# Stick-breaking attention: sigmoid(-z) scanned in SBUF instead of PSUM, and part of the weight splitting moved from VectorE to GpSimd

## The chip, the cores and the metric

The kernel runs on one core of a Trainium2 chip. Its metric is the device time of one execution, in microseconds (us), as the median of several executions; lower is better. Five engines matter: TensorE (PE in the profile; its weight loads are PEld), VectorE (DVE), ScalarE (ACT), GpSimd (POOL) and SyncE (SP), which issues the DMAs. Each takes its own instructions in a fixed order. Matmul results lie in PSUM (eight banks of 512 fp32 columns), everything else that the engines work on in SBUF.

## The reference

One layer of a streaming encoder, for 2048 prompt rows and for 128 sample rows (8 streams of 16) with a cache of 512 past positions. The input is normed, modulated and projected; two attention branches run side by side (A: differential attention; B: stick-breaking attention with 8 heads of 64); both are gated, merged, projected and normed. The change touches branch B alone:

```python
def stick_breaking_attention(q, k, v, qpos, kpos):
    z = jnp.einsum('bqhd,bkhd->bhqk', q, k) * (HEAD_DIM_B ** -0.5)
    mask = kpos[None, :] < qpos[:, None]
    log_1m = jnp.where(mask, jax.nn.log_sigmoid(-z), 0.0)
    log_a = jax.nn.log_sigmoid(z) + lax.cumsum(log_1m, axis=3, reverse=True) - log_1m
    a = jnp.where(mask, jnp.exp(log_a), 0.0)
    return jnp.einsum('bhqk,bkhd->bqhd', a, v)
```

The weight of key j is thus sigmoid(z_j) times the product of sigmoid(-z_i) over all later visible keys i. The kernel forms that product as a scan (a running product) from the last key to the first.

## The kernel before

**Order of the work.** A first phase (up to about 150 us) forms the modulated input and writes it to DRAM. The main loop (to about 1810 us) has eight units: four pairs of a branch-A unit (one head) and a branch-B unit (two heads). Each unit walks over the sample tile and then the 16 prompt tiles t = 0 to 15 of 128 rows. Tile t attends to t + 1 blocks of 128 keys, so late tiles are long. A last phase (to the end) does the sample attention, the branch and output projections and the final norm. One step of the main loop interleaves three streams: the projections of a tile some steps ahead (`project`, whose lead is reckoned by `LEAD` and by `duration`), the scores of the present tile (`scores`), and the product of weights and values of the tile two steps back (`pv`, `PV_LAG`). So towards the end of a B unit the projections are those of the next A unit. The framework then draws up each engine's order with a timeline of its own, from the order in which the program emits.

**One tile of a B unit.** For each of two heads `c`, chunks of 512 keys run from the last to the first. Per chunk, two matmuls (lines 639 and 640; on the diagonal also the mask, line 643) put z into a PSUM bank of the kind "s", of which there are three. `evacuate` (line 549) lets ScalarE write sigmoid(z) to the SBUF tile `seg["p"]` (line 562) and sigmoid(-z) back over z in PSUM (line 563). `stick` (line 606) lets VectorE scan that PSUM bank in reverse into the SBUF tile `seg["n"]` (line 616); the second operand of the scan is `zero_t`, one SBUF column read over and over. The bank is free once the scan has read it.

**Weights.** Every 1024 keys make a segment (`SEG` = 8 blocks), so tiles from t = 8 on have two segments for each head. Once a segment and the one after it are scanned, `stick_weights` (line 619) lets GpSimd multiply `p` by the scanned `n`, one column further (line 622). `turn` (line 565) then splits the product into two fp16 halves, written into the space of `n`: ScalarE copies the high half (line 572), VectorE subtracts to get the low half (line 573). SP issues a transposing DMA of both into `wt` (line 580), which the matmuls of `pv_block` (lines 700 and 701) read. The tiles `p` and `n` have six buffers each (`SC_BUFS`); a tile from t = 8 on takes four of each.

**Other users of these engines.** A projection for an A unit rotates queries and keys with three GpSimd instructions (lines 469, 471, 474) and splits them on VectorE (lines 463 and 295, from `rot` in SBUF); a projection for a B unit splits them straight from PSUM (`ps_mm`). GpSimd also multiplies each B output by its gate (line 683). SP's queue holds, among the transposes, the loads of the modulated input for the next projection (`hs`, line 405). In branch A, ScalarE and VectorE make the weights and GpSimd has no part in them.

## Time and profile before

| What | Value |
|---|---|
| Time, median of 3 runs | 2347.12 us (2343.01 to 2352.8) |
| Profiled execution, its own time | 2352.01 us |
| Its span, first to last instruction | 2350.2 us |
| Mean granted TensorE clock | 0.965 |
| PE busy in the span | 2124.9 us (90%) |
| DVE, ACT, POOL busy | 1725.1, 1644.4, 705.0 us |

The page gives each engine's busy time, then groups of instructions by source line: how many, how long in all, the mean of one, and how long the engine stood idle before them and what ended that. A busy PE may still be waiting inside, since matmuls are pipelined. Busy times of DVE and POOL include time in which an instruction has begun but is held up. A window view gives the busy times within a stretch of the span; a source view gives the shortest, median and longest duration of the instructions of one line.

### The profile page before, as it was taken

What the parts mean: (1) busy time and instruction counts of PE and PEld (TensorE: products, weight loads), DVE (VectorE), ACT (ScalarE), POOL (GpSimd) and SP (SyncE); (2) the same over time, 40 slices, a digit from 0 to 9 for tenths busy, and PEclk for the clock granted to TensorE, in tenths of its full rate; (3) what the DMA queues carried; (4) which work ended last, traced back from release to release, by engine and by line L of the source; (5) the groups of instructions that cost most, each with busy time, mean ns of one, the idle gap of its engine ahead of it and who ended that gap; (6) DMA issues with size and microseconds to landing.
All of it is one profiled execution on the core that took longest, in us unless ns stands there. A gap on an engine that the chain in (4) does not pass through costs nothing. (4 is left out here: it accounts for less than half of the span.)

```text
span 2350.2 us, 42700 instructions
## 1 busy us (share of the span) xinstructions
PE 2124.9 (90%) x15272; PEld 1144.5 (49%) x15272; DVE 1725.1 (73%) x3652; ACT 1644.4 (70%) x3260; POOL 705.0 (30%) x610
## 2 busy tenths in 40 slices
PE   5898899998999999899999979998996879988998
PEld 3554454444555445445545545554553344544443
DVE  4848866779875667978667797877688877777663
ACT  4557878787886778878677777866777656665541
POOL 1533012446300334731033474103335111221111
PEclk8999899999999999999999999999996989999999
DMA  9766759887895988867577787766687999999531
GB/s 334 252 203 177 165 127 263 180 188 163 207 227 131 213 199 189 175 175 191 139 188 175 186 171 185 192 146 149 142 175 162 288 238 250 237 249 243 157 103 48
DMA packets 834357, 445.34 MB, mean 189 GB/s; under 512 B 537210, under 2 KB 777130, under 8 KB 833632
## 3 DMA queue, kind: packets, MB, share of 16 engines
q1 hardware_dynamic: 833196, 442.24, 76.5%
q8 instruction: 119, 1.95, 0.3%
q14 instruction: 94, 0.77, 0.1%
q10 hardware_dynamic: 948, 0.39, 0.1%
HBM read 245.60 MB, written 69.24 MB: 134 GB/s over the span
## 5 line engine op out<-in xcount | busy, mean ns | idle before, releaser
L622 POOL TENSOR_TENSOR sc_p<-sc_p,sc_n 128x127 f32<-128x127 f32 (+7 forms) x192 | 314.2, 1640 | 834.8 <-DVE sc_n L616 812.5
L428 PE MATMUL ps_mm<-wb,hs 128*128 128x512 f16 x1632 | 412.1, 380 | 5.1 <-DMA hs<-hT_d 3.0
L428 PEld LDWEIGHTS <-hs 128*128 128x128 f16 x3120 | 275.8, 99 | 264.5 <-issue 14.8
L428 PE MATMUL ps_mm<-wa,hs 128*128 128x512 f16 x1488 | 377.7, 384 | 9.0 <-DVE qbuf L463 3.8
L616 DVE TENSOR_TENSOR_SCAN sc_n<-ps_s,sc_n,zero_t 128x512 f32<-128x512 f32 x192 | 245.5, 1279 | 80.8 <-ACT ps_s L119 77.5
L639 PE MATMUL ps_s<-k,qst 128*128 128x512 f16 (+3 forms) x640 | 227.5, 356 | 37.2 <-DVE sc_n L616 25.8
L573 DVE TENSOR_TENSOR sc_n<-sc_p,sc_n 128x128 f16<-128x128 f32 (+7 forms) x192 | 211.5, 1106 | 51.8 <-ACT sc_n L572 51.3
L504 PEld LDWEIGHTS <-hs 128*128 128x128 f16 x1632 | 155.6, 98 | 181.4 <-DVE qst L532 5.5
L119 ACT ACTIVATE sc_p<-ps_s,usc 128x512 f32<-128x512 f32 (+3 forms) x320 | 204.3, 638 | 35.3 <-PE ps_s L640 27.9
L640 PE MATMUL ps_s<-k,qst 128*128 128x512 f16 (+3 forms) x640 | 227.1, 356 | 0.0
L572 ACT CAST sc_n<-sc_p 128x128 f16<-128x128 f32 (+7 forms) x192 | 154.9, 811 | 78.9 <-POOL sc_p L622 76.0
L700 PE MATMUL ps_o<-v,wt 128*128 128x128 f16 x1088 | 172.2, 226 | 35.1 <-DMA wt<-sc_n 35.1
L119 ACT ACTIVATE ps_s<-ps_s,usc 128x512 f32<-128x512 f32 (+3 forms) x328 | 199.4, 608 | 0.0
L504 PE MATMUL ps_t<-wb,hs 128*128 128x512 f16 x816 | 192.9, 380 | 2.5 <-DVE qst L532 2.2
L504 PE MATMUL ps_t<-wa,hs 128*128 128x512 f16 x816 | 192.3, 381 | 3.1 <-DVE qst L532 2.2
L1341 PE MATMUL ps_o<-wo,wb 128*128 128x512 f16 x816 | 189.2, 386 | 4.0 <-ACT wb L1163 4.0
L701 PE MATMUL ps_o<-v,wt 128*128 128x64 f16 x1088 | 158.3, 198 | 0.0
L700 PEld LDWEIGHTS <-wt 128*128 128x128 f16 x1088 | 105.6, 101 | 100.1 <-DMA wt<-sc_n 46.4
L558 DVE TENSOR_SCALAR_CACHE_REDUCE sc_n<-ps_s,usc 128x512 f32<-128x512 f32 (+3 forms) x160 | 106.5, 666 | 42.2 <-PE ps_s L640 22.9
L616 DVE TENSOR_TENSOR_SCAN sc_n<-ps_s,zero_t 128x128 f32<-128x128 f32 (+3 forms) x128 | 104.2, 815 | 41.0 <-ACT ps_s L119 38.0
L558 DVE TENSOR_SCALAR_CACHE_REDUCE sc_p<-ps_s,usc 128x512 f32<-128x512 f32 (+3 forms) x160 | 106.4, 665 | 35.6 <-PE ps_s L640 26.1
L701 PEld LDWEIGHTS <-wt 128*128 128x128 f16 x1088 | 103.4, 101 | 54.5 <-issue 1.9
(358 smaller groups left out, 4531.3 us busy)
## 6 DMA issues: line engine op xcount, KB each, us to landing
hs<-hT_d SPq DMA_DIRECT2D x130, 512.0 KB, 4.4
g_d<-gt SPq DMA_DIRECT2D x68, 256.0 KB, 4.4
wb<-g_d SPq DMA_DIRECT2D x26, 512.0 KB, 5.7
out_dram<-pr SPq DMA_DIRECT2D x204, 64.0 KB, 2.4
o_d<-o SPq DMA_DIRECT2D x136, 64.0 KB, 2.0
hs<-o_d SPq DMA_DIRECT2D x17, 512.0 KB, 5.1
out_dram<-x SPq DMA_DIRECT2D x17, 512.0 KB, 2.8
wide<-in_w_ada_dram SPq DMA_DIRECT2D x8, 1024.0 KB, 7.8
```

What stands on the lines that cost most here:

```text
L119: i = S.activation(**kw)
L428: T.matmul(box["p"], box["h"][:, hi, k, :], U["w"][k][:, wi, :], start=(n == 0), stop=(n == 3 * KT - 1))
L504: T.matmul(box["g"][:, 0:gw], box["h"][:, hi, k, :], U["wg"][k // per][:, k % per, wi, :], start=(j == 0), stop=(j == 3 * KT - 1))
L558: V.tensor_scalar(out=dst[:, lo : lo + n], in0=p[:, 0:n], scalar1=sc_pos, scalar2=None, op0=ALU.mult, op1=ALU.max, accum_out=job["mx"][:, ...
L573: V.tensor_tensor(out=lo, in0=src, in1=hi, op=ALU.subtract)
L616: V.tensor_tensor_scan(out=dst[:, lo : lo + n][:, ::-1], data0=src[:, 0:n][:, ::-1], data1=zero_t[:, 0:1].to_broadcast([P, n]), initial=fi ...
L622: G.tensor_tensor(out=p[:, 0:m], in0=p[:, 0:m], in1=n[:, 1 : m + 1], op=ALU.mult)
L639: T.matmul(p[:, 0:n], qst[:, c, :], kk[:, c, 0:n], start=True, stop=False)
L640: T.matmul(p[:, 0:n], qst[:, 2 + c, :], kk[:, c, 0:n], start=False, stop=not diag)
L700: T.matmul(po[:, c * P : (c + 1) * P], wt[:, wj, :], vt[:, c, :, :], start=first, stop=False)
L701: T.matmul(po[:, c * P : c * P + 64], wt[:, nb + wj, :], vt[:, c, 0, :], start=False, stop=last)
L1341: T.matmul(po, st["y"][:, yi * 8 + k, :], wo[j * 4 + k // 2][:, wi, k % 2, :], start=(n == 0), stop=(n == 3 * KT - 1))
```

## The change

`evacuate` writes sigmoid(-z) to `seg["n"]` in SBUF, ahead of sigmoid(z), and no longer back into PSUM. `stick` loses its operand `src` and scans `seg["n"]` in place; its second operand is `zero_t` as before. In `turn`, for the second head (`c == 1`) of prompt tiles from t = 8 on, GpSimd subtracts the low half in place of VectorE. The same `evacuate` and `stick` serve the sample tile of the last phase, where the subtraction stays on VectorE.

```diff
         else:
 
+            act(out=seg["n"][:, lo : lo + n], in_=p[:, 0:n], func=AF.Sigmoid, scale=sc_neg)
             act(out=seg["p"][:, lo : lo + n], in_=p[:, 0:n], func=AF.Sigmoid, scale=sc_pos)
-            act(out=p[:, 0:n], in_=p[:, 0:n], func=AF.Sigmoid, scale=sc_neg)
...
             S.copy(out=hi, in_=src)
-            V.tensor_tensor(out=lo, in0=src, in1=hi, op=ALU.subtract)
+
+            (G if job["c"] == 1 and 8 <= job["t"] < NT else V).tensor_tensor(out=lo, in0=src, in1=hi, op=ALU.subtract)
...
-    def stick(seg, later, lo, n, src):
+    def stick(seg, later, lo, n):
...
-        V.tensor_tensor_scan(out=dst[:, lo : lo + n][:, ::-1], data0=src[:, 0:n][:, ::-1], data1=zero_t[:, 0:1].to_broadcast([P, n]),
+        x = dst[:, lo : lo + n][:, ::-1]
+        V.tensor_tensor_scan(out=x, data0=x, data1=zero_t[:, 0:1].to_broadcast([P, n]),
                              initial=first, op0=ALU.mult, op1=ALU.add)
...
-            stick(seg, later, ch * 512 - seg["lo"] * P, n, p)
+            stick(seg, later, ch * 512 - seg["lo"] * P, n)
...
-                    stick(seg, None, 512, P, pn[:, c * P : (c + 1) * P])
-                    stick(seg, None, 0, 512, pc)
+                    stick(seg, None, 512, P)
+                    stick(seg, None, 0, 512)
```

## The prediction

> **What bounds the kernel now.** I began with the page: engine totals and the costliest groups.

> ```profile
> PE 2124.9 (90%) x15272; PEld 1144.5 (49%) x15272; DVE 1725.1 (73%) x3652; ACT 1644.4 (70%) x3260; POOL 705.0 (30%) x610
> ...
> L639 PE MATMUL ps_s<-k,qst 128*128 128x512 f16 (+3 forms) x640 | 227.5, 356 | 37.2 <-DVE sc_n L616 25.8 <-DVE sc_p L558 7.8 <-DVE sc_n L558 3.1
> ...
> L119 ACT ACTIVATE sc_p<-ps_s,usc 128x512 f32<-128x512 f32 (+3 forms) x320 | 204.3, 638 | 35.3 <-PE ps_s L640 27.9 <-PE ps_s L643 6.9
> ...
> L119 ACT ACTIVATE ps_s<-ps_s,usc 128x512 f32<-128x512 f32 (+3 forms) x328 | 199.4, 608 | 0.0
> ```

> Over the whole span PE is busiest, and its waits for a PSUM bank that a scan still holds come to 25.8 us. An average hides stages, so next I asked for windows: tiles 8 to 12 of the first B unit, then tiles 13 to 15 of each of the four.

> ```profile
> 415.00:503.90 88.90, 84.20 (x569) 43.45 (x568) 62.41 (x102) 67.38 (x136) 33.33 (x26) 1.00 0.85 177
> 503.90:565.00 61.10, 51.20 (x421) 28.54 (x419) 59.13 (x66) 49.77 (x93) 41.95 (x30) 0.97 0.88 175
> 926.80:988.00 61.20, 50.54 (x424) 28.04 (x422) 58.76 (x65) 49.43 (x92) 44.67 (x32) 0.97 0.89 179
> 1341.40:1405.00 63.60, 52.71 (x451) 29.70 (x448) 60.56 (x65) 49.96 (x92) 44.63 (x32) 1.00 0.87 188
> 1754.30:1808.00 53.70, 32.14 (x283) 19.43 (x281) 51.16 (x61) 43.74 (x72) 33.69 (x20) 0.71 0.78 156
> ```

> Columns: length, then PE, PEld, DVE, ACT, POOL busy, granted clock. In the first row PE bounds (84 of 89). In the four late rows DVE does: 59.13 of 61.10, while PE idles 10 to 22 us each. The waits of the first late window, and PE's in the last, say the same:

> ```profile
> PE ps_s L639 <- DVE sc_n L616: 5.2, 7, 1.1
> PE ps_t L517 <- DVE k L295: 4.5, 3, 2.0
> ...
> PE ps_o L700 <- DMA wt<-sc_n: 14.9, 10, 3.2
> ```

> So the change is decided in these four stretches of three tiles, and there by DVE with POOL.

> **The rows that matter most: who blocks whom.** The source views (shortest, median, longest ns) of four kinds of DVE instruction:

> ```profile
> L616 DVE TENSOR_TENSOR_SCAN sc_n<-ps_s,sc_n,zero_t x192: 1265/1282/1285, 353.5 to 1801.2; 128x512 f32<-128x512 f32 x192
> L295 DVE SCALAR_TENSOR_TENSOR v<-ps_mm,usc,v x136: 318/344/352, 72.5 to 1747.7; 128x128 f16<-128x128 f32 x136
> L295 DVE SCALAR_TENSOR_TENSOR k<-rot,sq,k x68: 331/346/2089, 76.9 to 1503.0; 128x128 f16<-128x128 f32 x68
> L573 DVE TENSOR_TENSOR sc_n<-sc_p,sc_n x192: 266/1093/3052, 331.5 to 1808.3; 128x1024 f16<-128x1024 f32 x80, 128x128 f16<-128x128 f32 x16, 128x256 f16<-128x256 f32 x16, 128x384 f16<-128x384 f32 x16
> ```

> The first two read one tensor from PSUM and one from SBUF; they never vary. The last two read both from SBUF, and go from 346 to 2089 ns. The timelines of POOL and DVE show why (start, duration):

> ```profile
> 517.37 1.53 POOL L622 TENSOR_TENSOR sc_p<-sc_p,sc_n 128x767 f32<-128x767 f32 x1
> ...
> 525.63 1.77 POOL L622 TENSOR_TENSOR sc_p<-sc_p,sc_n 128x895 f32<-128x895 f32 x1 [0.30 <-DVE sc_n L616]
> ...
> 538.94 0.45 POOL L683 TENSOR_TENSOR o<-o,gt 128x128 f32<-128x128 f32 x1
> 539.92 2.76 POOL L622 TENSOR_TENSOR sc_p<-sc_p,sc_n 128x1024 f32<-128x1024 f32 x1 [0.54 <-DVE sc_n L616]
> 542.97 0.73 POOL L469 TENSOR_TENSOR rot<-pr,rope 128x256 f32<-128x256 f32 x1 [0.28 <-ACT pr L442]
> ...
> 546.44 2.00 POOL L622 TENSOR_TENSOR sc_p<-sc_p,sc_n 128x1023 f32<-128x1023 f32 x1 [1.73 <-DVE sc_n L616]
> ```
> ```profile
> 539.77 1.06 DVE L573 TENSOR_TENSOR sc_n<-sc_p,sc_n 128x896 f16<-128x896 f32 x1
> ...
> 546.73 2.79 DVE L573 TENSOR_TENSOR sc_n<-sc_p,sc_n 128x1024 f16<-128x1024 f32 x1
> ...
> 565.23 1.21 DVE L573 TENSOR_TENSOR sc_n<-sc_p,sc_n 128x1024 f16<-128x1024 f32 x1
> ```

> At 546.44 POOL is first and keeps its 2.00; the subtraction takes 2.79 in place of 1.21 and ends 1.08 after POOL. At 539.77 DVE is first; now POOL takes 2.76 and ends 1.85 after it. They take turns, whole instructions at a time, and hide some 0.14 us of each: a path into SBUF that both need. Today the scan does not need it. After the change it reads `sc_n` and `zero_t`, both in SBUF.

> [...]

> **Part 1: the scan in SBUF.** Its own length I keep: 1282 ns from PSUM, and the 128-wide splits take 344 from PSUM and 346 from SBUF. What it costs is its turn on the shared path. The windows of the scans' line and of the low halves' line (L573), DVE busy and count:

> ```profile
> 415.00:503.90 88.90, 35.12 (x33) 1.00 0.85 177
> 503.90:565.00 61.10, 28.50 (x24) 0.97 0.88 175
> ...
> 415.00:503.90 88.90, 17.75 (x20) 1.00 0.85 177
> 503.90:565.00 61.10, 19.43 (x11) 0.97 0.88 175
> 926.80:988.00 61.20, 21.36 (x12) 0.97 0.89 179
> 1341.40:1405.00 63.60, 24.41 (x12) 1.00 0.87 188
> 1754.30:1808.00 53.70, 15.49 (x12) 0.71 0.78 156
> ```

> The path's demand in one late window, each instruction at its undisturbed length less 0.14:
> - 24 scans: 28.5 - 3.4 = 25.1 (new on this path)
> - 12 POOL products: 8 x 2.00 + 2 x 1.77 + 2 x 1.53 = 22.6, less 1.7 = 20.9
> - 6 low halves left to DVE: 4 x 1.21 + 1.06 + 0.9 = 6.8, less 0.8 = 6.0
> - 15 rotations of the next A unit at 0.73: 8.9; its 10 splits at 0.34: 2.0; 4 output products at 0.45: 1.2

> **Part 2: six low halves on POOL.** DVE loses as many as it keeps. For POOL the nearest row subtracts fp16 from fp32 in the first phase:

> ```profile
> L1099 POOL TENSOR_TENSOR hp<-tmp,hp x40: 421/1156/1204, 42.2 to 141.2; 128x512 f16<-128x512 f32 x32, 128x128 f16<-128x128 f32 x8
> ```

> 421 ns for 128 and 1156 for 512 make about 2.1 us for 1024, beside 2.00 for a product. At the product's price six cost 11.3 - 0.8 = 10.5; at the dearer one 0.6 more a window.

> **Sum.** 25.1 + 20.9 + 6.0 + 8.9 + 2.0 + 1.2 + 10.5 = 74.6 us of demand against windows of 61.1, 61.2 and 63.6: +13.5, +13.4, +11.0. The last unit has no A projections behind it, 74.6 - 10.9 = 63.7 against 53.7: +10.0. In all **+48**. Tiles 8 to 12 of the first unit: scans 35.1 - 33 x 0.14 = 30.5, POOL at most 33.3, its new subtractions at most half as much again less 1.4 = 15.3, DVE's remaining low halves 17.75 / 2 = 8.9; 88.0 of 88.9, and less in truth, as those busy times include waiting. So full but not over: 0, at most +5 a unit.

> **What eases or adds to it.** A bank is now free after ScalarE's second sigmoid, so PE and ACT may run ahead of DVE until the six buffers are full: one and a half tiles, half a tile more than the one in work, about 10 us (61.1 / 3 / 2) a unit or 40 in all. But PE also waits for DVE's splits (4.5 above), which queue behind scans; I take half, -20. On POOL a low half must first wait for ACT's copy:

> ```profile
> 534.24 1.05 ACT L572 CAST sc_n<-sc_p 128x1024 f16<-128x1024 f32 x1 [0.68 <-POOL sc_p L622]
> ```

> Behind it in POOL's queue stand the next product and the rotations, for which ACT and DVE, then PE's transposes wait. Six times 1.05 is 6.3 a window, 25 in all, nothing if DVE fills the gap: I take half, +12. The transposing DMA starts later, and SP holds loads of `hs` behind it:

> ```profile
> SPq L580 <- DVE sc_n L573: 89.7, 55, 7.6
> ```
> ```profile
> L428 PE MATMUL ps_mm<-wb,hs 128*128 128x512 f16 x1632 | 412.1, 380 | 5.1 <-DMA hs<-hT_d 3.0
> ```

> PE lost 3.0 us to `hs` in that group of 1632, so a microsecond more is covered by the lead of those loads: 0; if it were not, this row would grow first. ScalarE's first sigmoid now ends in SBUF, 638 in place of 608 ns: 24 x 0.03 = 0.7 us a window on an engine with 49.8 of 61.1 busy, hidden by DVE's lag. That the scan may start one sigmoid sooner is worth nothing while DVE is late. The framework draws up every engine's order anew; no row prices that, and the width of the range has to hold it.

> [...]

> The profiled execution took 2352.0, so 2352.0 + 48 - 20 + 12 = 2392.0; it stands 4.9 above the median of the runs shown, 2347.1, so I forecast **2387**. Ends: 48 - 40 = +8 (all of the running ahead counts, no copy is waited for) gives 2355; 48 + 25 + 20 = +93 (no running ahead, every copy waited for, 5 lost in each unit's tiles 8 to 12) gives 2440.

> **The rivals.**
> 1. *The scan does not join the turns* (a one-column operand might not count as a stream). Then only part 2 acts where it was short. DVE sheds its six low halves with their waiting, 19.43 x 6 / 11 = 10.6, 10.7, 12.2 and 7.7 us, and POOL takes 11.3: 53.3, 56.0, 55.9 and 45.0 busy. POOL now bounds the first three windows: -7.8, -5.2, -7.7; in the last PE waits for transposes anyway (14.9), half of 7.7: -4. That is -25, **2322**. It decides if a scan beside a product stays at 1.28 us. For it: the scan never varied so far, and its one-column operand was in SBUF already. Against it: every quoted form with two SBUF tensors stretches.
> 2. *The turns are taken but absorbed*: PE runs ahead through freed banks, +8 at the most favourable, **2355** or less, within 0.5%. For it: the first window row, where PE bounds and DVE has 26 us to spare, and 5.2 us of bank waits that vanish. Against it: a queue cannot serve 74.6 us in 61, and the splits for PE's next projections stand in that queue.
> 3. *POOL becomes the bound as well* through copies it waits for: **2440** and more. For it: POOL's busy time of 42 to 45 with 11.3 to come. Against it: DVE can use the path meanwhile.
> 4. *The bank is not free sooner*, because ScalarE waits for a buffer of `n`, which the transposing DMA gives back later than now. Then the -20 is gone: 2407, inside the forecast's range.

> **How the numbers follow.** A difference under 0.5%, about 12 us, is what a measurement of this kernel can hardly tell from none. Forecast, 4 included (2360 to 2440): 0.62. Beyond 2440 (3): 0.04. Absorbed (2): 0.14. No turns for the scan (1): 0.20. So slower 0.66, same 0.14, faster 0.20. As both signs have weight, the range reaches from 2318, by rival 1, to 2440; it leaves out 0.04 above and some 0.1 below.

> **What would show it.** Right: the scan's source view goes from 1265/1285 to a longest near 3 us, stretched ones beside a POOL product; the products' and the new POOL subtractions' longest lies near 3 as well; windows of tiles 13 to 15 grow by 10 to 14 us each and DVE stays near 97% busy; the row <-DVE sc_n L616 vanishes from PE's waits, and <-DVE k L295 grows. Wrong: scans stay at 1.28 and the late windows shrink below 57 us (rival 1); scans stretch but PE is not idle longer (rival 2). What would make the forecast wrong altogether is a cost elsewhere: the windows of tiles 0 to 7, or the first and last phase, changing by more than a few us.

## The result and the profile after

The changed kernel took **2469.32 us** (median of 4 runs, 2462.56 to 2474.68) beside 2346.73 of the kernel before: a ratio of 1.0518, 95% interval 1.0484 to 1.0553. That is 122.6 us slower, where 40 had been forecast. The profiled executions differ by 116.0 (spans 2466.2 and 2350.2).

From the page of the changed kernel: engine totals, then groups (busy, mean ns | idle before, and what ended it).

```profile
PE 2166.4 (88%) x15272; PEld 1164.8 (47%) x15272; DVE 1854.3 (75%) x3588; ACT 1650.6 (67%) x3260; POOL 881.0 (36%) x674
...
L618 DVE TENSOR_TENSOR_SCAN sc_n<-sc_n,zero_t 128x512 f32<-128x512 f32 (+3 forms) x320 | 489.5, 1534 | 120.7 <-ACT sc_n L119 111.4
...
L641 PE MATMUL ps_s<-k,qst 128*128 128x512 f16 (+3 forms) x640 | 230.6, 361 | 24.5 <-ACT sc_p L119 11.8
L572 ACT CAST sc_n<-sc_p 128x128 f16<-128x128 f32 (+7 forms) x192 | 154.2, 807 | 142.7 <-POOL sc_p L624 142.1
```

The bank wait on the scan (25.8 before) is gone from the scores' row, as forecast. TensorE is busy 41.5 us longer with the same 15272 instructions, and it is idle for 74.5 more; together that is the 116.0. The scan's source view and those of the low halves (shortest, median, longest ns) show the turns:

```profile
L618 DVE TENSOR_TENSOR_SCAN sc_n<-sc_n,zero_t x320: 393/1284/3161, 327.0 to 1911.5; 128x512 f32<-128x512 f32 x88, 128x128 f32<-128x128 f32 x24, 128x256 f32<-128x256 f32 x24, 128x384 f32<-128x384 f32 x24
...
L574 POOL TENSOR_TENSOR sc_n<-sc_p,sc_n x64: 474/2128/3111, 428.3 to 1921.8; 128x1024 f16<-128x1024 f32 x36, 128x128 f16<-128x128 f32 x4, 128x256 f16<-128x256 f32 x4, 128x384 f16<-128x384 f32 x4
```

The longest scan is 3161 ns where none was over 1285. To place the loss I cut the trace at the first scan of a tile. First the kernel before, unit 1 (the first B unit): tiles 0 to 12, then 13 to 15 (from the first of their scans to the last; the columns are those of the prediction's windows, whose late ones had begun and ended a little differently).

```profile
328.36:503.87 175.51, 165.70 (x1104) 85.96 (x1103) 118.00 (x211) 138.49 (x297) 61.50 (x51) 0.99 0.88 204
503.87:562.80 58.93, 49.03 (x396) 27.12 (x394) 56.96 (x64) 49.73 (x92) 39.93 (x29) 0.97 0.87 175
```

And the changed kernel, the same for all four units:

```profile
327.01:511.01 184.00, 169.92 (x1104) 87.48 (x1103) 137.78 (x203) 138.22 (x296) 80.69 (x60) 0.96 0.83 194
511.01:581.96 70.95, 53.99 (x414) 30.34 (x411) 66.44 (x57) 48.43 (x89) 59.53 (x34) 0.90 0.70 145
773.30:964.15 190.85, 171.03 (x1098) 87.21 (x1096) 138.60 (x204) 137.52 (x294) 81.03 (x59) 0.96 0.78 182
964.15:1035.19 71.04, 54.27 (x417) 30.10 (x416) 69.15 (x56) 48.78 (x89) 60.93 (x34) 0.90 0.73 153
1224.24:1408.40 184.16, 166.99 (x1079) 85.41 (x1078) 137.95 (x205) 130.96 (x280) 81.17 (x59) 0.97 0.68 165
1408.40:1479.47 71.07, 55.46 (x436) 30.90 (x434) 68.83 (x56) 48.88 (x89) 60.95 (x34) 0.93 0.78 163
1664.50:1850.33 185.83, 163.32 (x1073) 84.20 (x1072) 144.58 (x212) 117.21 (x249) 84.36 (x59) 0.98 0.60 140
1850.33:1914.28 63.95, 30.32 (x257) 18.83 (x256) 62.26 (x49) 41.10 (x66) 47.36 (x22) 0.70 0.51 104
```

| us longer than before, by unit | 1 | 3 | 5 | 7 | sum |
|---|---|---|---|---|---|
| tiles 0 to 12 | 8.5 | 13.3 | 14.9 | 18.0 | 54.6 |
| tiles 13 to 15 | 12.0 | 11.8 | 8.8 | 15.8 | 48.4 |

The late windows cost 48.4, close to the 48 of the sum (part of that is luck, as the experiments show). Beside them stand 54.6 us in tiles 0 to 12, and DVE is not full there: 138 of 184. Of these, 29.5 fall in tiles 0 to 7, where the prediction had nothing, and 25.1 in tiles 8 to 12, where it had at most 20. The last 13.0 of the 116.0 lie outside these windows. TensorE's longest waits (us, times, longest), first in the kernel before:

```profile
PE ps_o L700 <- DMA wt<-sc_n: 35.1, 24, 5.2
...
PE ps_t L517 <- DVE k L295: 12.1, 11, 2.0
...
PE ps_mm L428 <- DMA hs<-hT_d: 4.5, 3, 2.6
...
PE ps_t L517 <- ACT gt L507: 3.3, 5, 1.1
```

And in the changed kernel:

```profile
PE ps_o L702 <- DMA wt<-sc_n: 50.8, 25, 7.2
PE ps_t L517 <- DVE k L295: 40.4, 14, 5.8
...
PE ps_mm L428 <- DMA hs<-hT_d: 20.9, 9, 4.3
PE ps_t L504 <- DVE qst L532: 16.1, 11, 3.4
...
PE ps_t L517 <- ACT gt L507: 11.9, 9, 3.1
```

The last of these can be followed in the timeline of tile 10, unit 1 (start, duration, wait before it):

```profile
461.88 1.89 POOL L574 TENSOR_TENSOR sc_n<-sc_p,sc_n 128x384 f16<-128x384 f32 x1
...
462.92 1.93 DVE L618 TENSOR_TENSOR_SCAN sc_n<-sc_n,zero_t 128x512 f32<-128x512 f32 x1
...
465.00 2.00 POOL L624 TENSOR_TENSOR sc_p<-sc_p,sc_n 128x1024 f32<-128x1024 f32 x1 [1.22 <-DVE sc_n L618]
...
467.03 1.04 ACT L572 CAST sc_n<-sc_p 128x1024 f16<-128x1024 f32 x1 [4.53 <-POOL sc_p L624]
467.98 0.68 ACT L507 ACTIVATE gt<-ps_t,usc 128x512 f32<-128x512 f32 x1
...
468.71 0.27 PE L517 MATMUL ps_t<-id,k 128*128 128x128 f16 x2 [3.07 <-ACT gt L507]
```

A low half delays a scan, the scan the product, the product ScalarE's copy; behind that copy stands the evacuation of the gate's bank, for which TensorE waits 3.07. The gate's matmuls had ended at 462.1, and the scan's own stretch in this chain is only 0.65 (1.93 for 1.28); the rest of the 3.07 is the place of the evacuation behind the copy. My first theory (A) was therefore: turns in all tiles, passed on through queues. Its rivals: part 2's longer GpSimd queue (B), the earlier release of banks and the engines' new order (D; the order alone is later F).

### The profile page after: what moved, and what is told of

Read it like the earlier page. It is cut to its first block, busy times and chain, and to the rows that moved or that the text cites. A ratio compares the mean times of both kernels' runs of the same rounds, so it can differ in the third digit from the quotient of the medians.

```text
span 2466.2 us, 42889 instructions
## 1 busy us (share of the span) xinstructions
PE 2166.4 (88%) x15272; PEld 1164.8 (47%) x15272; DVE 1854.3 (75%) x3588; ACT 1650.6 (67%) x3260; POOL 881.0 (36%) x674
## 5 line engine op out<-in xcount | busy, mean ns | idle before, releaser
L624 POOL TENSOR_TENSOR sc_p<-sc_p,sc_n 128x127 f32<-128x127 f32 (+7 forms) x192 | 326.1, 1702 | 736.4 <-DVE sc_n L618 578.1
L618 DVE TENSOR_TENSOR_SCAN sc_n<-sc_n,zero_t 128x512 f32<-128x512 f32 (+3 forms) x320 | 489.5, 1534 | 120.7 <-ACT sc_n L119 111.4
L428 PE MATMUL ps_mm<-wb,hs 128*128 128x512 f16 x1632 | 419.2, 387 | 14.7 <-DMA hs<-hT_d 11.7
L428 PEld LDWEIGHTS <-hs 128*128 128x128 f16 x3120 | 278.6, 100 | 284.0 <-issue 25.0
L428 PE MATMUL ps_mm<-wa,hs 128*128 128x512 f16 x1488 | 383.1, 389 | 12.0 <-DMA hs<-hT_d 9.2
L641 PE MATMUL ps_s<-k,qst 128*128 128x512 f16 (+3 forms) x640 | 230.6, 361 | 24.5 <-ACT sc_p L119 11.8
L572 ACT CAST sc_n<-sc_p 128x128 f16<-128x128 f32 (+7 forms) x192 | 154.2, 807 | 142.7 <-POOL sc_p L624 142.1
L119 ACT ACTIVATE sc_n<-ps_s,usc 128x512 f32<-128x512 f32 (+3 forms) x320 | 203.2, 635 | 34.1 <-PE ps_s L642 16.2
L702 PE MATMUL ps_o<-v,wt 128*128 128x128 f16 x1088 | 178.6, 231 | 50.9 <-DMA wt<-sc_n 50.8
L119 ACT ACTIVATE sc_p<-ps_s,usc 128x512 f32<-128x512 f32 (+3 forms) x320 | 204.6, 639 | 0.0
L702 PEld LDWEIGHTS <-wt 128*128 128x128 f16 x1088 | 110.5, 105 | 119.6 <-DMA wt<-sc_n 63.1
L574 DVE TENSOR_TENSOR sc_n<-sc_p,sc_n 128x1024 f16<-128x1024 f32 (+7 forms) x128 | 150.6, 1178 | 21.7 <-ACT sc_n L572 21.7
L574 POOL TENSOR_TENSOR sc_n<-sc_p,sc_n 128x128 f16<-128x128 f32 (+7 forms) x64 | 135.0, 2110 | 31.5 <-ACT sc_n L572 31.5
L558 DVE TENSOR_SCALAR_CACHE_REDUCE sc_n<-ps_s,usc 128x512 f32<-128x512 f32 (+3 forms) x160 | 106.3, 665 | 42.9 <-PE ps_s L642 29.6
L469 POOL TENSOR_TENSOR rot<-pr,rope 128x256 f32<-128x256 f32 x68 | 68.6, 1009 | 192.1 <-ACT pr L442 137.5
L1351 POOL TENSOR_TENSOR x<-m,x 128x512 f32<-128x512 f32 x34 | 49.7, 1464 | 240.0 <-DVE m L1347 156.7
```

Of the source, the lines that this page charges most:

```text
L119: i = S.activation(**kw)
L428: T.matmul(box["p"], box["h"][:, hi, k, :], U["w"][k][:, wi, :], start=(n == 0), stop=(n == 3 * KT - 1))
L572: S.copy(out=hi, in_=src)
L574: (G if job["c"] == 1 and 8 <= job["t"] < NT else V).tensor_tensor(out=lo, in0=src, in1=hi, op=ALU.subtract)
L618: V.tensor_tensor_scan(out=x, data0=x, data1=zero_t[:, 0:1].to_broadcast([P, n]), initial=first, op0=ALU.mult, op1=ALU.add)
L624: G.tensor_tensor(out=p[:, 0:m], in0=p[:, 0:m], in1=n[:, 1 : m + 1], op=ALU.mult)
```

## The experiments

**The parts alone.** Part 1 alone is the changed kernel with

```diff
-            (G if job["c"] == 1 and 8 <= job["t"] < NT else V).tensor_tensor(out=lo, in0=src, in1=hi, op=ALU.subtract)
+            V.tensor_tensor(out=lo, in0=src, in1=hi, op=ALU.subtract)
```

and part 2 alone the kernel before with the reverse edit.

> Part 1 alone: the scan in SBUF, every low half left on VectorE. Theory A (the scan takes turns with GpSimd, and through GpSimd's late products ScalarE's queue and then TensorE are held up): nearly the whole loss stays. The path's demand in a late window falls by the low halves' difference only (six at 1.9 to six at 1.1), so 65 to 110 us over the kernel before, 2410 to 2455; scans' longest near 3 us, high-half copies of ScalarE waiting for the product 110 to 140 us in all. Rival B (the loss in tiles 0 to 12 comes from GpSimd's longer queue, part 2): only the late windows lose, at most 48 us, so 2370 to 2395, and tiles 0 to 12 stand as before.

> Part 2 alone: sigmoid(-z) and the scan as in the kernel before (scan from PSUM), but from tile 8 on GpSimd subtracts the low halves of the second head's weights. Theory A (the scan's turns are the loss): no loss; VectorE sheds six low halves in each late window, and by the first rival of the prediction the time is 2322, or with copies waited for up to 2347. Rival B (GpSimd's longer queue is the loss): 30 us or more slower than before, 2377 and up, with the high-half copies' wait on GpSimd's products grown as in the changed kernel (142).

Part 1 took 2443.52 (ratio 1.0383, 1.0358 to 1.0407): 91 slower, as A had it. Part 2 took 2369.73 (1.0066, 1.0043 to 1.0090): 17 slower, and neither theory had that. Its late windows did shrink, by 18 in all, but all the rest grew by 39. Whether these 39 belong to the part or to the engines' new order, the runs below settle.

**Do the two SBUF operands make the turns?** A pair with two score banks; in the second kernel the freed bank holds the scan's zero.

```diff
-    BANKS = {"mm": 2, "s": 3, "t": 1, "o": 2}
+    BANKS = {"mm": 2, "s": 2, "t": 1, "o": 2}
...
+    zero_p = ps.tile([P, 512], F32, tag="z", name="ps_z", bufs=1)
+    V.memset(zero_p[:, 0:1], 0.0)
...
-... data1=zero_t[:, 0:1].to_broadcast([P, n]),
+... data1=zero_p[:, 0:1].to_broadcast([P, n]),
```

> The changed kernel with two score banks in place of three, to free one bank; a control for the next run. The bank is free after the second sigmoid, so two may do: both theories expect the changed kernel's time or up to 30 us more (2465 to 2500), scans' longest near 3 us.

> As the control, but the scan's second operand, the repeated zero, is a column in PSUM (in the freed bank), so the scan reads one tensor from SBUF and one from PSUM and writes SBUF. Theory A (two SBUF operands make it take turns, the repeated column counting as one): the scan is back at 1.26 to 1.30 us, shortest to longest, though it reads and writes sc_n in SBUF, and the time falls by 60 us or more against the control. Rival C (reading and writing the same SBUF tensor, or any SBUF read of a long tensor beside GpSimd, makes it wait): scans still reach near 3 us, and the time is the control's within 15 us.

The control took 2520.33, the kernel with the zero in PSUM 2426.04. In the two traces TensorE, ScalarE and GpSimd run the same instructions in the same order (VectorE has the one memset more). The scan's source view, control first:

```profile
L618 DVE TENSOR_TENSOR_SCAN sc_n<-sc_n,zero_t x320: 398/1284/3140, 346.6 to 1966.2; 128x512 f32<-128x512 f32 x88, 128x128 f32<-128x128 f32 x24, 128x256 f32<-128x256 f32 x24, 128x384 f32<-128x384 f32 x24
```
```profile
L620 DVE TENSOR_TENSOR_SCAN sc_n<-sc_n,ps_z x320: 395/1268/1282, 346.7 to 1876.4; 128x512 f32<-128x512 f32 x88, 128x128 f32<-128x128 f32 x24, 128x256 f32<-128x256 f32 x24, 128x384 f32<-128x384 f32 x24
```

With one column moved to PSUM no scan is stretched, and 94 us go. So here a column repeated from SBUF counts as a second SBUF operand, and rival C falls. The 94 hold for the order of this pair.

**The same with three banks: a probe that brought its own wait.** To keep three score banks, the zero was put into an unused column of an output bank; in two further kernels the SBUF column stayed in tiles 13 to 15, or in 0 to 12, and a last one took part 1 alone.

```diff
+        zero = o_ring[0][:, 511:512]           (the two: zero_t[:, 0:1] if 13 <= t < NT, or if t < 13)
...
-... data1=zero_t[:, 0:1].to_broadcast([P, n]),
+... data1=zero.to_broadcast([P, n]),
```

> The changed kernel whole, with its three score banks, but the scan's repeated zero is one unused column of an output bank in PSUM. Theory A (the turns of the scan with GpSimd are the loss, in all tiles): scans 1.26 to 1.30 us throughout, and the time falls by 85 us or more against the changed kernel, to 2345 to 2385. Rival D (a good part is lost by what else the change does, the bank that is given back sooner and the new order of the engines): 2400 or more although no scan is stretched.

> As the run before, but in tiles 13 to 15 the scan's zero is the SBUF column again, so scans take turns in these tiles alone. Theory A: the late windows alone give the prediction's 48 us and some half-clock time on top, 45 to 75 over the run before; tiles 0 to 12 as in the run before.

> The reverse: SBUF column in tiles 0 to 12, PSUM column from 13 on. Theory A (in tiles 0 to 12 the path is not full, but late products, splits and transfers stop TensorE there all the same): 40 to 70 over the run with PSUM everywhere. The prediction's step (these tiles lose nothing, as the path has time to spare): at most 10 over it.

> Part 1 alone without the turns: sigmoid(-z) and the scan in SBUF, the scan's zero in PSUM, every low half on VectorE. Theory A: the score bank comes free one scan sooner and nothing is paid for it: 2325 to 2350, at or under the kernel before. Rival D: 2370 or more.

They took 2487.70, 2481.62, 2468.67 and 2513.13, far off A's numbers; D's (2400 or more, and 2370 or more) were met, but the waits in the first of them show another cause. VectorE's, then TensorE's:

```profile
DVE sc_n L630 <- PE ps_o L715: 81.5, 51, 4.3
```
```profile
PE ps_o L714 <- DVE sc_n L630: 39.0, 32, 3.4
```

No scan was stretched (1282 ns at most), but scans now waited 51 times for the matmuls that write other columns of that bank, and the matmuls 32 times for them. These four therefore decide nothing about the turns or about D.

**One order for both.** The framework draws up each engine's order anew for every kernel. So the next four hold it fixed: an edge without a wait from each instruction to the next of the order wanted, on all five engines (the two sigmoids of a chunk stand in each other's place, as the change has them; the 64 low halves that change engine find their own place).

```diff
+    for each engine, for each instruction i of the order kept, last before it:
+        tc.add_manual_dep(i, last.name, NOSYNC, reason="order kept")
```

> The changed kernel, made to keep the order of the kernel before on every engine (edges without a wait fix each engine's order; the 64 low halves on GpSimd find their own place). Theory A (the turns of the scan with GpSimd are the bulk, at 94 of 122 by the pair with the zero in PSUM; the rest is the engines' new order): 85 to 110 over the kernel before, 2430 to 2460, some 15 to 35 under the changed kernel. Rival F (the order is half or more of it): 2410 or less. Rival G (the order is nothing): 2465 to 2475.

> Part 1 alone (scan in SBUF, every low half on VectorE) in the order of the kernel before, the same on all engines to the last instruction. So what differs is the scan's operands and the earlier release of the bank. Theory A: 70 to 95 over the kernel before (part 1 alone in its own order was 90 over). Rival F: 50 or less.

> Part 2 alone (from tile 8 on GpSimd subtracts the second head's low halves; the scan from PSUM) in the order of the kernel before. In its own order it was 17 slower, with late windows 18 shorter and more TensorE time at half clock. Theory A (those 17 come of the new order, and the part itself saves VectorE time in the late windows): 2335 to 2352. Rival H (the part itself costs, through low halves that wait in GpSimd's queue): 2360 or more.

> The kernel before with the order of the changed kernel on every engine, and nothing else of the change. Theory A: 15 to 40 slower than the kernel before, with waits for hs and for the gate's bank in tiles 0 to 12 as in the changed kernel. Rival G (the order is nothing): within 8 of it.

| kernel | own order, us more | order of the kernel before, us more (ratio, 95%) |
|---|---|---|
| part 1 | 90.6 | 49.5 (1.0212, 1.0181 to 1.0243) |
| part 2 | 16.8 | -4.9 (0.9987, 0.9972 to 1.0002) |
| both | 122.6 | 67.9 (1.0286, 1.0262 to 1.0311) |

The kernel before, in the order of the changed kernel, took 2382.64: 30.0 more (1.0131, 1.0105 to 1.0157).

The new order alone costs 30.0 where no scan takes turns, and 54.7 on top of the change (48.9 if the two medians, 2469.32 and 2420.47, are taken directly; the kernel before took 2346.73 beside the one and 2352.62 beside the other). So the order is 40 to 45 in a hundred of the loss: for both parts together neither A's range (2430 to 2460) nor F's (2410 or less) was met. Part 2's 17 were order: without it the part makes no difference that can be measured, and that run is also the nearest there is to a control of the edges themselves. In the order of before the windows of unit 1 are

```profile
328.30:504.98 176.68, 165.59 (x1100) 85.83 (x1098) 136.01 (x202) 138.34 (x296) 83.61 (x60) 0.99 0.85 202
504.98:576.76 71.78, 54.00 (x413) 30.57 (x414) 66.55 (x59) 50.03 (x93) 59.62 (x34) 0.88 0.70 145
```

The late windows are +12.9, +13.4, +11.3 and +17.4 longer, 54.9 in all; tiles 0 to 12 only +1.2, -0.6, +4.0 and +3.0. Cut the same way, the profiled executions give, in us more than the kernel before over all four units:

| kernel | tiles 0 to 7 | 8 to 12 | 13 to 15 | the rest | sum |
|---|---|---|---|---|---|
| changed kernel | 29.5 | 25.1 | 48.4 | 13.0 | 116.0 |
| both parts, order of before | 4.8 | 2.8 | 54.9 | 0.4 | 62.9 |
| kernel before, order of the changed kernel | 18.6 | 4.4 | -11.1 | 16.1 | 28.0 |

The last two rows do not add up to the first: 25 us come only when both are there. Two of TensorE's waits do part. The one for hs is 2.1 in the second row's kernel and 16.0 in the third's, so it goes with the order; the one for VectorE's splits is 49.4 and 10.3, so it goes with the change.

**Late tiles or all tiles, in that order.** The scan in SBUF under a condition on the tile, from PSUM otherwise; part 2 whole.

```diff
+            inner = 13 <= job["t"] < NT        (the other kernel: job["t"] < 13)
...
+                             data0=x if inner else src[:, 0:n][:, ::-1],
```

> The whole of part 2, but the scan in SBUF in tiles 13 to 15 alone (elsewhere from PSUM, as before), in the order of the kernel before on every engine. With the scan from PSUM everywhere this order took 2348, with it in SBUF everywhere 2420. Theory A (the late windows are over-full, the others are not): 45 to 65 over the kernel before, 2398 to 2418. Rival I (once the order is the same, the cost is spread over all tiles): 2385 or less.

> The reverse in the same order: the scan in SBUF in tiles 0 to 12 alone. Theory A, and the prediction's own step (at most 5 a unit in tiles 8 to 12, nothing in 0 to 7): 0 to 20 over the kernel before, 2350 to 2372. Rival I: 2385 or more.

They took 2406.46 (1.0243, 1.0223 to 1.0263) and 2359.26 (1.0043, 1.0028 to 1.0058): +56.8 and +9.6, both as A had it, and their sum is the 67.9 of both to within 2. Rival I falls. Unit 1 of each:

```profile
329.64:505.65 176.01, 165.27 (x1100) 85.70 (x1098) 114.33 (x202) 138.03 (x296) 73.63 (x60) 0.99 0.86 203
505.65:577.42 71.77, 52.81 (x404) 29.72 (x405) 66.55 (x59) 49.98 (x93) 59.61 (x34) 0.88 0.71 145
```
```profile
328.17:506.34 178.17, 165.89 (x1104) 86.10 (x1103) 135.59 (x202) 138.72 (x297) 83.56 (x60) 0.99 0.85 201
506.34:562.20 55.86, 48.36 (x409) 27.21 (x407) 49.01 (x59) 49.09 (x92) 47.28 (x34) 1.00 0.87 184
```

In tiles 0 to 12 VectorE is 21.3 us longer busy with turns (135.59 against 114.33) and the stretch only 2.2 longer: in this order something else covers the turns, and in the changed kernel's it does not.

**What in the new order costs?** In the kernel before with the new order, the wait for hs is 16.0 where it was 4.5:

```profile
PE ps_mm L431 <- DMA hs<-hT_d: 16.0, 8, 4.4
```

So each load of hs was set two places earlier in SyncE's queue, the changed kernel's order being otherwise kept.

```diff
 SyncE's kept order, for each load of hs (L405):
-    ..., transfer, transfer, load of hs, ...
+    ..., load of hs, transfer, transfer, ...
```

> The changed kernel in its own order on every engine, except that each load of hs stands two places earlier in SyncE's queue, which takes it past one transposing transfer or store that waits. Theory J (much of what the new order costs in tiles 0 to 12 are loads of hs that stand behind waiting transfers; TensorE waits 20.9 for them there, 16.4 more than in the kernel before, and half as much again is lost to the half clock): 10 to 30 faster than the changed kernel, 2440 to 2460, and that wait at most 10. Rival K (those waits only take the place of others): within 8 of 2469, the wait for the gate's bank or for the splits grown by as much.

2546.61 (1.0850, 1.0824 to 1.0876): some 75 slower than the changed kernel, which neither J nor K had. TensorE's wait for hs did go, from 20.9 to 2.0, but SyncE now stands longer at the load, until a gate's matmuls give an hs buffer back, and the transposing transfers behind it are late. SyncE's row of the changed kernel, then of this one, and below them this one's rows of TensorE's waits:

```profile
SPq L405 <- PE ps_t L504: 78.5, 25, 8.1
```
```profile
SPq L408 <- PE ps_t L507: 163.4, 41, 12.5
```
```profile
PE ps_o L705 <- DMA wt<-sc_n: 90.5, 37, 7.2
...
PE ps_mm L431 <- DMA hs<-hT_d: 2.0, 1, 2.0
```

The wait for wt stood at 50.8 in the changed kernel. So two places in one queue are worth more than the whole late-window effect, and a wait that goes with the order need not be what the order costs. Which engine's order carries the 30 and the 55 stays **open**: no run changed the order of one engine other than SyncE.

## Why the prediction was wrong

The scan's turns, the mechanism of the forecast, were right; the step that failed is the engines' new order, which the sum put at nothing. Step by step:

- **The scan joins the turns** (an inference from the two subtracting forms, as both of its operands would lie in SBUF; no row of the kernel before showed it): right, shown by the pair with the zero in PSUM (3140 ns at the longest with the column in SBUF, 1282 without). Rival 1 is out.
- **"In all +48"**: right in the order of before for three units: the late windows grew by 12.9, 13.4 and 11.3 against 13.5, 13.4 and 11.0. The last unit's 10.0 was mis-sized: it measured 17.4, and 14.6 with part 1 alone in that order (62.75 against 48.19), so the excess comes mostly with the scan; why stays open. In the changed kernel the 48.4 is in part luck: there the new order by itself shortens these windows by 11.1.
- **"Full but not over: 0, at most +5 a unit"** for tiles 8 to 12, and the windows of tiles 0 to 7 unchanged: right in the order of before (7.6 in four units; 9.6 by its own run), wrong in the kernel that was asked about (54.6, of which 29.5 in tiles 0 to 7). The prediction had named a change there as the sign of a cost elsewhere, and so it was.
- **"-20" for running ahead**: did not come. The bank wait went, yet in the order of before TensorE's wait for splits rose from 12.1 to 49.4, and the splits stand behind the scans in VectorE's queue:

```profile
PE ps_o L705 <- DMA wt<-sc_n: 62.6, 32, 5.7
PE ps_t L520 <- DVE k L298: 49.4, 13, 7.3
```

- **"+12" for copies that GpSimd waits for**: not shown. With SBUF scans part 2 adds 18.4 (67.9 less 49.5); without them it gives 4.9. But by the prediction's own prices six low halves take 10.5 of the shared path on GpSimd and 6.0 on VectorE, 4.5 a window or 18 in all, and that leaves nothing of the 18.4 for the copies.
- **"The framework draws up every engine's order anew; no row prices that, and the width of the range has to hold it"**: this step failed. A term with no row was put at nothing in the sum and left to a range that had 53 above the forecast for everything. The order cost 30 by itself and 49 to 55 with the change. In the order of before the change stood at 2420, inside the range, between the 2407 without running ahead and the 2440 with every copy waited for. "A microsecond more is covered by the lead of those loads" held in that order (the wait for hs is 2.1 there, 4.5 in the kernel before) and failed in the new one (20.9).
- **The other rivals.** The bank did come free sooner (4 is out), and the turns were not absorbed (2: in the order of before the two parts still cost 67.9). The measured time lies where rival 3 stood, 2440 and more, but its mechanism did not bring it there: part 1 alone, with no low half on GpSimd, took 2443.52, and GpSimd is busy for 60 of 71 in the late windows where VectorE is busy for 66 to 69.
- **TensorE's clock was in no term.** The trace's clock records have 28 stretches at half clock before, 46 after; TensorE is busy for 121.9 and 209.2 us in them. The 512-wide matmuls of line 428 start 426 to 427 ns apart there and 216 at full clock (medians, in either trace), so half of that time is lost. Half of the difference, 43.6, is as much as the growth of its busy time (41.5). For each microsecond that TensorE was idle longer, the kernel took 1.6 longer (116.0 by 74.5).

## What to carry to other kernels

When an edit changes what is ready when, price the new order as well as the operands: run the change in the old order and the old kernel in the new order, and see what the two effects are apart and what they do to each other (here 67.9, 30.0 and some 25). The operand repeated from one SBUF column made the scan here take turns with GpSimd (3140 ns at the longest), so count it as a full SBUF operand; with it in PSUM no scan here was stretched (1282 ns at the longest), but in a bank that TensorE wrote too the scans waited for matmuls instead (81.5 us, 51 times). And where a path is full in a few windows only, a sum of demand against those windows' lengths forecast three of the four here well, but it says nothing of the queues elsewhere.

## What the runs showed of the hardware

The pair with two score banks shows what a second operand in SBUF does to a scan beside GpSimd's work, even if it is one repeated column: 3140 ns at the longest with the column in SBUF, 1282 with it in PSUM. In the changed kernel 148 of the 320 scans took over a tenth longer than the shortest of their shape, and each of the 148 overlapped an instruction of GpSimd.
